# The seven block products of an FFN pair in another order, with the weight sums queued later

## The chip, the cores and the metric

One kernel runs on one core of a Trainium2 chip. The metric is the device time of one execution in microseconds; before the change it is 2068.62 us, the median of three executions (2066.19 to 2069.09). The core has five engines that run side by side, each in its own order: TensorE (PE in the profile, its weight loads PEld), VectorE (DVE), ScalarE (ACT), GpSimd (POOL) and SyncE (SP, whose queue issues most transfers from memory). They wait for each other by semaphores.

## The reference

The kernel computes one inference step of a two-layer network on 128 context tokens and 512 latent tokens with 1024 features. Each layer has a mixer (state space and attention in the first layer, a gated linear recurrence in the second) and then a gated convolutional feed-forward part, the FFN, which the change touches:

```
def conv_ffn(h, w_up, conv_w, conv_b, w_down):
    u = dwconv_centred(h @ w_up, conv_w, conv_b)     # width 3, along the tokens
    val, g = jnp.split(u, 2, axis=-1)
    return (jax.nn.silu(g) * val) @ w_down
...
    xp = xp + gp_f * conv_ffn(modulate(rmsnorm(xp, norm_ffn_g[l]), sp_f, sc_f), *fw)
    xs = xs + gs_f * conv_ffn(modulate(rmsnorm(xs, norm_ffn_g[l]), ss_f, scs_f), *fw)
```

w_up is 1024 x 5632 and w_down 2816 x 1024, all in float32. Modulation vectors (shift, scale, gate) come from a further product with w_mod.

## The kernel before, in words

The 644 token columns (128 of context, a gap of 4, 512 of latents) lie along the free dimension, the features on the partitions. Every product keeps float32 accuracy by splitting each operand into a high part (rounded to fp32r) and a low part (the rest) and adding three matmuls: high by high, high by low, low by high (mm3, L472 to L474). A weight block of 128 output features is loaded as a tile wraw, its high part whi is cast on ACT (L113), its low part wlo is subtracted on POOL in pieces of 256 columns (L118).

The 22 blocks of the value half of w_up and the 22 of the gate half are taken in pairs: pair j is block j of either half. The first two are ordinary products. The other 20 of each FFN are computed by up_pair with seven products of half size in place of eight. The block a is cut into a11 and a12 (its first and last four groups of 128 input features), the block b likewise, and DVE forms sums of them: add_up (L141 to L144) writes s2, s3 and s4 into one tile wsum and s1 over the first half of b. ACT casts the high parts shi of s2, s3, s4, and POOL (for s2) or DVE (for s3 and s4) subtracts the low parts slo. The token side has its own sums T1 to T4 (names t24h, t3h and so on), made once. Then

p1 = a11 B11, p2 = a12 B21, p3 = s4 B22, p4 = a22 T4, p5 = s1 T1, p6 = s2 T2, p7 = s3 T3,

each of them twelve matmuls of 128 x 322, into half of a PSUM tile called wide (128 x 1024; one product lies at column 0, the next at column 512, and then a new tile is taken from three that go round). In the kernel before, the order is p1, p6 | p5, p2 | p7, p4 | p3, where a bar stands between tiles. Copies on ACT (L1602 for p1, L1607 for p5) and additions on DVE (L1604, L1609, L1611, L1614, L1616) and POOL (L1612, L1615) put the seven together into u (value) and g (gate). After that come the convolution (ACT L1551, then two fused operations on DVE at L319 for each of u and g), SiLU (ACT L1567), the product of value and gate (L1562) and its split into hidh and hidl (L509, L513).

The order on PE in each FFN is: two pairs, then six times a down block and three pairs, then the last down block. A down block is eight products of three hidden tiles with w_down, and DVE adds each to the running state X at L319. In the first FFN products for the modulation vectors of the second layer stand between the pieces (M.step).

The program is written out by Python before it runs: the position of each instruction on its engine is the moment at which the Python code emits it. A counter k.clock advances by one with every three matmuls of a half product (tick); after(n, f) emits f when the counter is n further on, and W.ahead(1) emits the next piece of weight work when there are buffers for it. Three wraw, three whi/wlo and four shi/slo buffers go round; wsum is one. pump() asks for the next weight block as soon as the code has given a wraw buffer free. The class Weights holds the lists of pieces for a pair: before, add_up, block a, s2, s3, block b, s4.

Of the kernel before, what the change touches and what calls it, by code (L numbers as in the profile page):

```python
# [44 lines left out]
AHEAD = 3  # L45
N_HID, N_FT = 4, 5
# [37 lines left out]
class Weights:  # L84
# [6 lines left out]
    def __init__(self, nc, pool, items):  # L91
        self.nc, self.pool, self.items = nc, pool, items
        self.loaded = self.freed = self.queued = self.next = 0
        self.raw, self.parts, self.pieces = {}, {}, []
        self.n_raw, self.n_part, self.n_sum = 3, 3, 4
        self.n_w = self.n_s = 0
        self.sums = self.over = None
        self.limit = len(items)

    def pump(self):  # L100
        while self.loaded < min(len(self.items), self.freed + self.n_raw, self.limit):
            ap, kt, w, _ = self.items[self.loaded]
            t = self.pool.tile([128, 8, 128], F32, name="wraw", tag="wraw", bufs=self.n_raw)[:, :kt, :w]
            self.nc.sync.dma_start(t, ap.rearrange("(k p) c -> p k c", p=128))
            self.raw[self.loaded] = t
            self.loaded += 1
# [16 lines left out]
    def block(self, i):  # L123
        raw = self.raw.pop(i)
        if self.items[i][3] == "held":
            hi, lo = (self.over.tile(list(raw.shape), F32R, name=f"{p}{i}") for p in ("hi", "lo"))
            self.nc.scalar.copy(hi, raw)
            for k0 in range(0, raw.shape[1], 2):
                q = slice(k0, min(raw.shape[1], k0 + 2))
                self.nc.gpsimd.tensor_sub(lo[:, q], raw[:, q], hi[:, q].bitcast(F32))  # L130
            self.parts[i] = hi, lo
        else:
            low = self.nc.vector if self.items[i][3] == "vector" else self.nc.gpsimd
            self.parts[i] = self.split(self.pool, raw, "w", self.n_part, low)
        self.freed += 1

    def add_up(self, i):
        a, b = self.raw[i], self.raw[i + 1]
# [11 lines left out]
    def ahead(self, n=100):  # L150
        self.pump()
        for _ in range(n):
            if not self.pieces:
# [4 lines left out]
                if kind == "pair":  # L158
                    if not self.sums or self.loaded < i + 2:
                        return  # L160
                    self.pieces = [(0, lambda: self.add_up(i)), (1, lambda: self.block(i)),
                                   (2, lambda: self.sum_part(i, 0)), (2, lambda: self.sum_part(i, 1)),
                                   (1, lambda: self.block(i + 1)), (2, lambda: self.sum_part(i, 2))]
# [6 lines left out]
            what, f = self.pieces[0]  # L170
            if (what == 1 and self.n_w == self.n_part) or (what == 2 and self.n_s == self.n_sum):
                return
# [6 lines left out]
    def upto(self, i):  # L179

        was = None
        while was != (self.queued, len(self.pieces)) and (self.queued <= i or self.pieces):
            was = self.queued, len(self.pieces)
            self.ahead(1)

    def get(self):
        for _ in range(8):
            if self.next not in self.parts:
                self.ahead(1)
# [4 lines left out]
    def get_pair(self):  # L194
        i = self.next
        while self.queued < i + 2 or (self.queued == i + 2 and self.pieces):
            self.ahead(1)
# [45 lines left out]
def tile_hybrid_step(ctx: ExitStack, tc: tile.TileContext, a, o):  # L243
# [193 lines left out]
    k.bg, k.events, k.clock, k.count = [], [], 0, 0  # L437

# [1060 lines left out]
    def ffn(l, final=None):  # L1499
        with ExitStack() as st:  # L1500
# [78 lines left out]
            def up_pair(j):  # L1579
# [20 lines left out]
                p6 = product(s2, T2, 0, 1)  # L1600
                g, u = tmp(), tmp()
                nc.scalar.copy(g[:, L], p1)  # L1602
                p5 = product(s1, T1)
                nc.vector.tensor_add(u[:, R], p6, g[:, L])  # L1604
                p2 = product(a12, B21, 1)
# [3 lines left out]
                nc.vector.tensor_add(u[:, L], p2, g[:, L])  # L1609
                p4 = product(a22, T4, 1)  # L1610
                nc.vector.tensor_add(g[:, R], p7, u[:, R])  # L1611
                nc.gpsimd.tensor_add(u[:, R], u[:, R], x5)  # L1612
                p3 = product(s4, B22, 0, 1)
                nc.vector.tensor_add(g[:, L], p4, g[:, R])  # L1614
# [369 lines left out]
```

## Time and profile before

| | us |
|---|---|
| median of three executions | 2068.62 |
| the profiled execution | 2074.41 |
| its span, first to last instruction | 2071.4 |
| PE busy | 1885.9 (91%) |
| DVE busy | 1421.0 (69%) |
| POOL busy | 1157.9 (56%) |
| ACT busy | 967.5 (47%) |
| mean granted clock of PE | 0.961 of full speed |

The times in rows are from one execution, the profiled one, counted in microseconds from the start of its span. A row of the timeline gives start, duration, engine, line, operation, output and inputs, and in brackets the idle time of the engine before it and the instruction that ended that idle time. The matmuls of PE overlap one another, so that the distance of two starts, not the duration, is what one costs. Forty pairs run: twenty in the first FFN (about 823 to 1267 us) and twenty in the second (about 1601 to 2019 us).

### The profile page before, as it was taken

Reading aid. Unit: us, or ns where it says so; the run is one execution under the profiler, and the core shown is the slowest. Engines: PE = TensorE matmul, PEld = TensorE weight load, DVE = VectorE, ACT = ScalarE, POOL = GpSimd, SP = SyncE. Lnnn points to the kernel's source line nnn. Section 1 sums busy time; section 2 is a strip of 40 time slices with the busy share of each in tenths; the row PEclk is TensorE's granted clock in tenths of the full one; section 3 lists DMA queues with packets and bytes.
Section 4 is the critical chain, followed back from the end, with each engine's and each line's share of the span. In section 5 each row is a group of like instructions: output and inputs, shape, how many; then the busy total and the mean of one; then the engine's idle time right before and its main releaser. Section 6 shows DMA issues by size and latency. Waiting matters only on the chain. (4 is left out here: it accounts for less than half of the span.)

```text
span 2071.4 us, 33556 instructions
## 1 busy us (share of the span) xinstructions
PE 1885.9 (91%) x12601; PEld 1721.9 (83%) x12601; DVE 1421.0 (69%) x2446; ACT 967.5 (47%) x1679; POOL 1157.9 (56%) x1496
## 2 busy tenths in 40 slices
PE   6878889999999999899999998988789899999997
PEld 4667768888887889788899998977689899999986
DVE  3477764665666347777777776778857777777875
ACT  3454443455545325433434434587726443444445
POOL 3235544333325344566567776468665578776772
PEclk9889999999999999999999999999889899999999
DMA  9554432112113351345543222212121122222221
GB/s 255 179 167 145 143 117 84 49 50 56 39 49 115 100 165 59 97 156 184 154 125 101 85 85 81 59 39 56 41 62 52 46 68 83 85 80 70 62 82 71
DMA packets 255576, 196.58 MB, mean 95 GB/s; under 512 B 13837, under 2 KB 233816, under 8 KB 255288
## 3 DMA queue, kind: packets, MB, share of 16 engines
q1 hardware_dynamic: 249784, 183.94, 29.6%
q0 software_dynamic: 2528, 7.13, 1.5%
q10 hardware_dynamic: 3104, 3.38, 0.5%
q8 instruction: 99, 1.62, 0.3%
q14 instruction: 61, 0.50, 0.1%
HBM read 187.50 MB, written 6.92 MB: 94 GB/s over the span
## 5 line engine op out<-in xcount | busy, mean ns | idle before, releaser
L118 POOL TENSOR_TENSOR wlo<-wraw,whi 128x256 fp32r<-128x256 f32 (+1 forms) x803 | 678.3, 874 | 560.1 <-ACT whi L113 496.3
L472 PE MATMUL wide<-hhi,whi 128*128 128x322 f32 (+4 forms) x1072 | 358.4, 334 | 25.0 <-DVE X L319 16.8
L473 PE MATMUL wide<-hlo,whi 128*128 128x322 f32 (+4 forms) x1072 | 344.2, 321 | 8.2 <-DVE hlo L513 8.0
L474 PE MATMUL wide<-hhi,wlo 128*128 128x322 f32 (+4 forms) x1072 | 341.6, 319 | 3.6 <-POOL wlo L118 3.6
L113 ACT CAST whi<-wraw 128x1024 fp32r<-128x1024 f32 (+1 forms) x259 | 217.2, 840 | 148.4 <-PE wide L474 72.0
L472 PEld LDWEIGHTS wide<-hhi,whi 128*128 128x128 f32 x1072 | 211.2, 197 | 44.1 <-ACT shi L113 16.9
L472 PE MATMUL gh<-hhi,whi 128*128 128x322 f32 (+3 forms) x688 | 232.5, 338 | 8.7 <-ACT zt L1179 8.7
L473 PEld LDWEIGHTS wide<-hlo,whi 128*128 128x128 f32 x1072 | 210.6, 197 | 14.1 <-DVE hlo L513 10.0
L473 PE MATMUL gh<-hlo,whi 128*128 128x322 f32 (+3 forms) x688 | 217.1, 315 | 1.3 <-DVE hlo L513 1.0
L474 PE MATMUL gh<-hhi,wlo 128*128 128x322 f32 (+3 forms) x688 | 216.3, 314 | 0.0
L474 PEld LDWEIGHTS wide<-hhi,wlo 128*128 128x128 f32 x1072 | 211.0, 197 | 4.2 <-POOL wlo L118 4.2
L319 DVE SCALAR_TENSOR_TENSOR ft<-ft,PC 128x643 f32<-128x643 f32 x160 | 167.2, 1066 | 42.7 <-ACT ft L1551 40.8
L472 PE MATMUL wide<-hidh,whi 128*128 128x322 f32 (+2 forms) x600 | 191.3, 319 | 1.1 <-DVE ft L1609 1.1
L473 PE MATMUL wide<-hidl,whi 128*128 128x322 f32 (+2 forms) x600 | 186.9, 311 | 0.8 <-DVE hidl L513 0.8
L474 PE MATMUL wide<-hidh,wlo 128*128 128x322 f32 (+2 forms) x600 | 186.9, 311 | 0.0
L472 PEld LDWEIGHTS gh<-hhi,whi 128*128 128x128 f32 (+1 forms) x688 | 131.8, 192 | 34.1 <-issue 21.2
L319 DVE SCALAR_TENSOR_TENSOR X<-wide,modc,X 128x128 f32<-128x128 f32 (+3 forms) x276 | 128.1, 507 | 30.2 <-PE wide L474 30.2
L1551 ACT ACTIVATE ft<-ft,PC 128x644 f32<-128x644 f32 x80 | 73.9, 926 | 145.6 <-DVE ft L1616 135.5
L473 PEld LDWEIGHTS gh<-hlo,whi 128*128 128x128 f32 (+1 forms) x688 | 131.5, 191 | 2.4 <-DVE hlo L513 1.2
L474 PEld LDWEIGHTS gh<-hhi,wlo 128*128 128x128 f32 (+1 forms) x688 | 131.3, 191 | 0.6
L113 ACT CAST shi<-wsum 128x512 fp32r<-128x512 f32 x120 | 72.8, 617 | 123.0 <-DVE wsum L143 111.4
L472 PEld LDWEIGHTS wide<-hidh,whi 128*128 128x128 f32 x600 | 113.6, 189 | 14.5 <-issue 6.6
(380 smaller groups left out, 4632.1 us busy)
## 6 DMA issues: line engine op xcount, KB each, us to landing
wraw<-in_ffn_w_up_dram SPq DMA_DIRECT2D x88, 512.0 KB
mraw<-in_w_mod_dram SPq DMA_DIRECT2D x80, 512.0 KB
wraw<-in_ssd_attn_w_in_dram SPq DMA_DIRECT2D x42, 512.0 KB
wraw<-in_ffn_w_down_dram SPq DMA_DIRECT2D x96, 192.0 KB
E<-ad SPq DMA_DIRECT2D x16, 640.0 KB
mraw<-in_w_mod_dram SPq DMA_DIRECT2D x32, 256.0 KB
wraw<-in_ssd_attn_w_out_dram SPq DMA_DIRECT2D x16, 512.0 KB
wraw<-in_lru_w_in_dram SPq DMA_DIRECT2D x16, 512.0 KB
```

The costliest lines, as they stand in the source:

```text
L113: self.nc.scalar.copy(hi, src)
L118: low.tensor_sub(lo[:, q], src[:, q], hi[:, q].bitcast(F32))
L319: nc.vector.scalar_tensor_tensor(out, in0, scalar, in1, op0=op0, op1=op1, **kw)
L472: nc.tensor.matmul(ps[:whi.shape[-1], p0:p0 + c1 - c0], whi, xhi[:, c0:c1], start=start, stop=False)
L473: nc.tensor.matmul(ps[:whi.shape[-1], p0:p0 + c1 - c0], whi, xlo[:, c0:c1], start=False, stop=False)
L474: nc.tensor.matmul(ps[:whi.shape[-1], p0:p0 + c1 - c0], wlo, xhi[:, c0:c1], start=False, stop=stop)
L1551: after(at, lambda: nc.scalar.activation(out, u, AF.Identity, scale=par(cw, 2 * NF + t), bias=par(cb, t)))
```

## The change

The seven products are computed in the order p1, p2 | p4, p6 | p5, p7 | p3. The copy of p1 is emitted right after p1, the addition of p2 right after p2, the copy of p5 right after p5, and the addition of p4 before p3. In Weights, the pieces of a pair come as block a, add_up, block b, s2, s3, s4; add_up is emitted at the earliest 12 ticks after the request for block b (LANDING), unless the pair is needed at once; the buffer of block a is given free in add_up.

```
+LANDING = 12
...
             self.raw[self.loaded] = t
+            self.asked[self.loaded] = self.clock()
             self.loaded += 1
...
-    def block(self, i):
-        raw = self.raw.pop(i)
+    def block(self, i, whole=True):
+        raw = self.raw.pop(i) if whole else self.raw[i]
...
+        self.freed += whole
+
+    def add_up(self, i):
+        a, b = self.raw.pop(i), self.raw[i + 1]
         self.freed += 1
-
-    def add_up(self, i):
-        a, b = self.raw[i], self.raw[i + 1]
...
-                    if not self.sums or self.loaded < i + 2:
+                    if not self.sums or self.loaded <= i:
                         return
-                    self.pieces = [(0, lambda: self.add_up(i)), (1, lambda: self.block(i)),
-                                   (2, lambda: self.sum_part(i, 0)), (2, lambda: self.sum_part(i, 1)),
-                                   (1, lambda: self.block(i + 1)), (2, lambda: self.sum_part(i, 2))]
+                    self.pieces = [(1, lambda: self.block(i, False)), (0, lambda: self.add_up(i)),
+                                   (1, lambda: self.block(i + 1)), (2, lambda: self.sum_part(i, 0)),
+                                   (2, lambda: self.sum_part(i, 1)), (2, lambda: self.sum_part(i, 2))]
...
             what, f = self.pieces[0]
+            if what == 0:
+                last = self.queued - 1
+                if self.loaded <= last or (not now and self.clock() < self.asked[last] + LANDING):
+                    return
...
+    W.clock = lambda: k.clock
...
                 p1 = product(a11, B11)
-                p6 = product(s2, T2, 0, 1)
                 g, u = tmp(), tmp()
                 nc.scalar.copy(g[:, L], p1)
-                p5 = product(s1, T1)
+                p2 = product(a12, B21, 1)
+                nc.vector.tensor_add(u[:, L], p2, g[:, L])
+                p4 = product(a22, T4)
+                p6 = product(s2, T2, 0, 1)
                 nc.vector.tensor_add(u[:, R], p6, g[:, L])
-                p2 = product(a12, B21, 1)
+                p5 = product(s1, T1, 1)
                 x5 = pool.tile([128, NT2], F32, name="x5", tag="x5", bufs=1)
                 nc.scalar.copy(x5, p5)
                 p7 = product(s3, T3, 0, 1)
-                nc.vector.tensor_add(u[:, L], p2, g[:, L])
-                p4 = product(a22, T4, 1)
                 nc.vector.tensor_add(g[:, R], p7, u[:, R])
                 nc.gpsimd.tensor_add(u[:, R], u[:, R], x5)
+                nc.vector.tensor_add(g[:, L], p4, g[:, R])
                 p3 = product(s4, B22, 0, 1)
-                nc.vector.tensor_add(g[:, L], p4, g[:, R])
                 nc.gpsimd.tensor_add(g[:, R], g[:, R], x5)
                 nc.vector.tensor_add(u[:, R], u[:, R], p3)
                 nc.gpsimd.memset(g[:, NP:S0], 0.0)
```

The remaining hunks pass now=True where a pair or a block is needed at once. No instruction is added or taken away on any engine; only places change. Line numbers shift by three to nine: after the change the casts are L116, POOL's differences L121, DVE's L123, add_up L145 to L148, the fused operation L327, mm3 L481 to L483, the convolution L1560, the copy of p1 L1610, the addition of p2 L1612, the copy of p5 L1618, the additions of p7, p4 and p3 L1620, L1622 and L1625.

On PE, in the second pair of the last group of three, this is where p1 ends and the next product begins. Before (the names end in numbers of their own; hhi4 is the fifth block of the tokens' high part, and what a row waits for stands in brackets):

```order
L472 MATMUL wide_20096<-hhi3_77,whi_19948 128x322
L473 MATMUL wide_20096<-hlo3_85,whi_19948 128x322
L474 MATMUL wide_20096<-hhi3_77,wlo_19949 128x322
L472 MATMUL wide_20096<-t24h0_15659,shi_19969 128x322
L473 MATMUL wide_20096<-t24l0_15663,shi_19969 128x322
L474 MATMUL wide_20096<-t24h0_15659,slo_19970 128x322 [waits Pool_49]
L472 MATMUL wide_20096<-t24h1_15660,shi_19969 128x322
L473 MATMUL wide_20096<-t24l1_15664,shi_19969 128x322
```

and now:

```order
L481 MATMUL wide_20089<-hhi3_77,whi_19943 128x322
L482 MATMUL wide_20089<-hlo3_85,whi_19943 128x322
L483 MATMUL wide_20089<-hhi3_77,wlo_19944 128x322
L481 MATMUL wide_20089<-hhi4_78,whi_19943 128x322 [waits Activation_49]
L482 MATMUL wide_20089<-hlo4_86,whi_19943 128x322
L483 MATMUL wide_20089<-hhi4_78,wlo_19944 128x322 [waits Pool_49]
L481 MATMUL wide_20089<-hhi5_79,whi_19943 128x322
L482 MATMUL wide_20089<-hlo5_87,whi_19943 128x322
```

Behind p1 stood p6, whose weights are the sums shi; now p2 stands there, in the same tile wide as p1, and its first matmul carries a wait for ACT: the instruction waited for is the copy of p1 (L1610), which reads that tile. The first matmul of p7 has such a wait for the copy of p5 (L1618).

On DVE, in a steady group of the second FFN, the end of a down block, where X takes the products of its fifth, sixth and seventh output block (the eighth comes later). Before:

```order
L319 SCALAR_TENSOR_TENSOR X_73<-wide_17784,modc1_113,X_73 128x128
L319 SCALAR_TENSOR_TENSOR X_73<-wide_17784,modc1_113,X_73 128x512
L141 TENSOR_TENSOR wsum_17812<-wraw_17749,wraw_17782 128x512
L142 TENSOR_TENSOR wraw_17782<-wraw_17782 128x512
L143 TENSOR_TENSOR wsum_17812<-wraw_17782,wraw_17749 128x512
L144 TENSOR_TENSOR wsum_17812<-wraw_17749,wsum_17812 128x512
L319 SCALAR_TENSOR_TENSOR X_73<-wide_17817,modc1_113,X_73 128x128
L319 SCALAR_TENSOR_TENSOR X_73<-wide_17817,modc1_113,X_73 128x512
L120 TENSOR_TENSOR slo_17853<-wsum_17812,shi_17852 128x512
L319 SCALAR_TENSOR_TENSOR X_73<-wide_17856,modc1_113,X_73 128x128
L319 SCALAR_TENSOR_TENSOR X_73<-wide_17856,modc1_113,X_73 128x512
```

and now:

```order
L327 SCALAR_TENSOR_TENSOR X_73<-wide_17784,modc1_113,X_73 128x128
L327 SCALAR_TENSOR_TENSOR X_73<-wide_17784,modc1_113,X_73 128x512
L327 SCALAR_TENSOR_TENSOR X_73<-wide_17812,modc1_113,X_73 128x128
L327 SCALAR_TENSOR_TENSOR X_73<-wide_17812,modc1_113,X_73 128x512
L145 TENSOR_TENSOR wsum_17840<-wraw_17749,wraw_17782 128x512
L146 TENSOR_TENSOR wraw_17782<-wraw_17782 128x512
L147 TENSOR_TENSOR wsum_17840<-wraw_17782,wraw_17749 128x512
L148 TENSOR_TENSOR wsum_17840<-wraw_17749,wsum_17840 128x512
L327 SCALAR_TENSOR_TENSOR X_73<-wide_17847,modc1_113,X_73 128x128
L327 SCALAR_TENSOR_TENSOR X_73<-wide_17847,modc1_113,X_73 128x512
L123 TENSOR_TENSOR slo_17883<-wsum_17840,shi_17882 128x512
L123 TENSOR_TENSOR slo_17887<-wsum_17840,shi_17886 128x512
```

The four operations of add_up for the next pair (tile wsum) have moved behind one more addition to X, that of the sixth block. The first tile wide of the next pair is the one that the sixth block's product lay in, its second the seventh's, its third the eighth's.

On ACT, from the last casts ahead of the first copy of a group of three pairs to the copy of the second pair. Before:

```order
L113 CAST whi<-wraw 128x1024
L113 CAST shi<-wsum 128x512
L1602 COPY ft<-wide 128x322
L113 CAST shi<-wsum 128x512
L1607 COPY x_18665<-wide 128x322
L113 CAST whi<-wraw 128x1024
L113 CAST shi<-wsum 128x512
L113 CAST whi<-wraw 128x1024
L1551 ACTIVATE ft<-ft,PC 128x644
L113 CAST shi<-wsum 128x512
L1551 ACTIVATE ft<-ft,PC 128x644
L1602 COPY ft<-wide 128x322
```

and now:

```order
L116 CAST whi<-wraw 128x1024
L1610 COPY ft<-wide 128x322
L116 CAST whi<-wraw 128x1024
L116 CAST shi<-wsum 128x512 x2
L1618 COPY x_18688<-wide 128x322
L116 CAST shi<-wsum 128x512
L116 CAST whi<-wraw 128x1024
L1560 ACTIVATE ft<-ft,PC 128x644 x2
L1610 COPY ft<-wide 128x322
```

The casts of the pair's second block (whi) and of its sums (shi) stand in another order around the copies. The copy of p1 of the second pair stands behind both convolutions of the first pair, before and now.

## Rows read from the trace of the kernel before

**Rows 1.** The page, busy time, share and instructions of each engine.

```profile
PE 1885.9 (91%) x12601; PEld 1721.9 (83%) x12601; DVE 1421.0 (69%) x2446; ACT 967.5 (47%) x1679; POOL 1157.9 (56%) x1496
```

**Rows 2.** Windows: length, then busy (count) PE, PEld, DVE, ACT, POOL, clock, DMA.

```profile
1791.00:1854.00 63.00, 59.68 (x397) 58.98 (x397) 49.39 (x68) 26.12 (x42) 46.01 (x56) 1.00 0.26 76
...
896.00:967.00 71.00, 68.80 (x498) 61.48 (x499) 54.85 (x90) 27.89 (x44) 46.95 (x59) 1.00 0.52 161
```

**Rows 3.** Waits: engine, line, what was waited for: total us, times, longest.

```profile
ACT ft L1551 <- DVE ft L1616: 135.5, 40, 4.4
...
PE wide L472 <- DVE X L319: 22.6, 16, 2.7
```

**Rows 4.** Timeline of PE, second FFN, a steady group of three pairs.

```profile
1790.99 0.39 PE L472 MATMUL wide<-hhi,whi 128*128 128x322 f32 x1 [2.14 <-DVE X L319]
...
1799.41 0.39 PE L472 MATMUL wide<-t3h,shi 128*128 128x322 f32 x1 [1.05 <-DVE X L319]
...
1804.70 0.30 PE L474 MATMUL wide<-hhi,slo 128*128 128x322 f32 x1
...
1815.82 0.39 PE L472 MATMUL wide<-hhi,shi 128*128 128x322 f32 x1 [0.15 <-DVE ft L1604]
...
1817.52 0.31 PE L474 MATMUL wide<-hhi,slo 128*128 128x322 f32 x1
```

**Rows 5.** Timeline of DVE, the same group.

```profile
1786.41 0.92 DVE L141 TENSOR_TENSOR wsum<-wraw 128x512 f32<-128x512 f32 x1 [3.88 <-DMA wraw<-in_ffn_w_up_dram]
...
1789.85 1.00 DVE L319 SCALAR_TENSOR_TENSOR X<-wide,modc,X 128x128 f32<-128x128 f32 x2
...
1807.91 0.48 DVE L1616 TENSOR_TENSOR ft<-ft,wide 128x322 f32<-128x322 f32 x1
...
1815.20 0.48 DVE L1604 TENSOR_TENSOR ft<-wide,ft 128x322 f32<-128x322 f32 x1
...
1822.12 0.49 DVE L1616 TENSOR_TENSOR ft<-ft,wide 128x322 f32<-128x322 f32 x1 [1.11 <-POOL ft L1612]
```

**Rows 6.** Timeline of PE, first FFN, fourth and sixth group.

```profile
1109.45 0.39 PE L472 MATMUL wide<-t3h,shi 128*128 128x322 f32 x1 [0.55 <-DVE X L319]
...
1227.35 0.61 PE L472 MATMUL wide<-hhi,whi 128*128 128x322 f32 x1 [2.71 <-DVE X L319]
```

**Rows 7.** Timeline of PE and ACT, a copy that waited only for PE.

```profile
1636.59 0.31 PE L474 MATMUL wide<-hhi,wlo 128*128 128x322 f32 x1
...
1636.94 0.43 ACT L1607 COPY x<-wide 128x322 f32<-128x322 f32 x1 [0.39 <-PE wide L474]
```

**Rows 8.** Timeline of ACT, the group of rows 4.

```profile
1790.28 1.04 ACT L113 CAST whi<-wraw 128x1024 fp32r<-128x1024 f32 x1
...
1791.75 1.05 ACT L113 CAST whi<-wraw 128x1024 fp32r<-128x1024 f32 x1
...
1808.43 0.93 ACT L1551 ACTIVATE ft<-ft,PC 128x644 f32<-128x644 f32 x1 [4.14 <-DVE ft L1616]
...
1809.77 0.92 ACT L1551 ACTIVATE ft<-ft,PC 128x644 f32<-128x644 f32 x1
1810.60 0.41 ACT L1602 COPY ft<-wide 128x322 f32<-128x322 f32 x1
```

**Rows 9.** Timeline of PE and DVE, end of the second pair of the second FFN.

```profile
1641.92 0.31 PE L474 MATMUL wide<-hhi,slo 128*128 128x322 f32 x1
...
1642.34 0.49 DVE L1616 TENSOR_TENSOR ft<-ft,wide 128x322 f32<-128x322 f32 x1 [0.83 <-PE wide L474]
```

**Rows 10.** Windows of PE alone: length, busy (matmuls), clock, DMA share, GB/s.

```profile
1728.12:1731.50 3.38, 3.38 (x14) 0.57 0.54 158
1791.00:1794.40 3.40, 3.40 (x23) 1.00 0.54 154
```

**Rows 11.** Timeline of PE and ACT, first pair of the second FFN.

```profile
1607.92 0.64 PE L472 MATMUL wide<-t24h,shi 128*128 128x322 f32 x1 [4.21 <-ACT shi L113]
...
1615.61 0.42 ACT L1602 COPY ft<-wide 128x322 f32<-128x322 f32 x1
```

More of the change, by code (lines that the diff above doesn't have):

```diff
@@ L98, in __init__ @@
         self.limit = len(items)
+        self.clock, self.asked = (lambda: 0), {}
     def pump(self):
@@ L148, in sum_part, with ahead @@
             self.split(self.sums, self.s[:, n], "s", self.n_sum, self.nc.vector if n else self.nc.gpsimd))
-    def ahead(self, n=100):
+    def ahead(self, n=100, now=False):
         self.pump()
@@ L183, in upto @@
             was = self.queued, len(self.pieces)
-            self.ahead(1)
+            self.ahead(1, True)
     def get(self):
@@ L188, in get @@
             if self.next not in self.parts:
-                self.ahead(1)
+                self.ahead(1, True)
         p = self.parts.pop(self.next)
@@ L196, in get_pair @@
         while self.queued < i + 2 or (self.queued == i + 2 and self.pieces):
-            self.ahead(1)
+            self.ahead(1, True)
         return self.get(), self.get(), self.parts.pop((i, "s"))
```

## The prediction

> **What bounds the kernel now.** I read the page's busy times first: PE is busy 91% of the span, every other engine 69% or less [rows 1]. So the end is set by how many matmuls PE issues and by the gaps between them; the change leaves the number as it is. Next the windows: a steady group of the second FFN (a down block and three pairs) takes 63 us, with 397 matmuls and PE busy for 59.68 us; DVE is busy 49.39, POOL 46.01, ACT 26.12 us [rows 2]. One matmul costs 59.68 / 397 = 0.15 us, a product of twelve 1.8 us. So about 3.5 us a group can be won, and no other engine is full; a queue matters only where PE waits for it. Then the waits: PE waited 22.6 us for DVE's additions to X, 16 times [rows 3]. The timeline gives the places. PE stands 2.14 us before the first pair of the group and 1.05 us before its p7, both for X [rows 4]; the addition that ends the first stands behind add_up, which had waited 3.88 us for its block to land [rows 5]. With the slower first matmul each costs 0.15 us more: 2.3 and 1.2. Before p3 of the second pair 0.3 us go [rows 4]. Together 3.8 us a group. Last the ACT queue: its convolutions waited 135.5 us for the last addition of the pair before, 40 times, 4.4 us at most [rows 3]. Nothing on PE waited for that, so far.
>
> **What goes.** The additions of X for the sixth and the eighth block now stand ahead of add_up, and p3's tile waits for the addition of p2, which has four products' time. All three stalls should go: -3.8 us for each of the six groups of the second FFN. In the first FFN the last three groups lost less: 0.55 us at one p7, up to 2.71 us at a start [rows 6]. The third group there lies between; with the slow clock behind the two longer stalls (below) I take 3.2 on the mean. In its first three groups, with modulation products in between, PE is idle 71 - 68.8 = 2.2 us [rows 2], and I count 1.2 of it.
>
> **What comes.** The order shows the point that decides: p1 and p2 share a tile, and so do p5 and p7. The copies of p1 and p5 are now emitted between the two, so the first matmul of p2 waits on a semaphore for ACT's copy, and that of p7 likewise. Before, PE waited only at the borders of tiles, where the reader was a product or two behind. Two new waits a pair, 80 in all.
>
> The least one costs: a copy starts 0.35 us after the last matmul's start and takes 0.43 [rows 7]; PE starts 0.14 us after its releaser ends (1815.20 + 0.48 = 1815.68, against 1815.82) [rows 4, 5]. That is 0.92 us from the last matmul, of which 0.15 would have passed anyway: 0.77 us. For p7, with ACT nearly free, I take 0.8 to 0.85.
>
> For p2 the queue of ACT counts. In the first pair of a group the copy stands behind the casts of the sums and of the next pair's block a. These ended at 1792.80, with one cast of 1.04 us among them [rows 8] that is now done earlier: 1791.8. The copy and the restart add 0.4 and 0.14: 1792.3. PE without its start stall would begin at 1790.99 - 2.3 = 1788.7 and end p1 at 1790.5. Stall 1.8 us, and 0.3 for the low parts of the sums, which POOL now takes up behind block b.
>
> In the second and third pair the copy stands behind both convolutions of the pair before, and these behind its last addition on DVE. From that addition's end to the copy's end it is 1808.39 to 1811.01 here, with a cast of 0.6 between the two convolutions that has moved away [rows 5, 8]; so 0.04 + 0.84 + 0.84 + 0.42 + 0.14 = 2.3 us to PE's restart, less the 1.8 of p1: the stall is the lateness of the last addition plus 0.5. That lateness is 1808.39 - 1804.85 = 3.54 us in the first pair and 1822.61 - 1817.67 = 4.94 in the second [rows 4, 5]; at its least 1642.83 - 1642.07 = 0.76 [rows 9]. It should shrink, since add_up of the next pair but one no longer stands in DVE's queue ahead of it, but POOL's addition still stands behind the two pieces of a sum's low part. For the first pair I take 2.5, in the middle; for the second, with a lighter queue, 1.25. The stalls of p2 are then 3.0 and 1.75.
>
> A group: 1.8 + 0.3 + 0.8 + 3.0 + 0.85 + 1.75 + 0.85 = 9.35 us added. Least: 0.77 + 2 x 1.26 + 3 x 0.77 = 5.6. Most, with the old lateness: 1.8 + 0.3 + 0.8 + 4.0 + 0.85 + 5.4 + 0.85 = 14.0, and 2.3 of the start stall kept.
>
> The transfers: a block is asked for in another place by one piece, on a queue with a share of 0.26 [rows 2]. I count nothing; pairs of 12.5 us cover it, and if a landing is late, it delays add_up and is in the "most".
>
> **The sum.** Second FFN: 6 x (9.35 - 3.8) = 33.3. First FFN, last three groups: 3 x (9.35 - 3.2) = 18.5. First three: the modulation products between pairs ((68.8 - 59.7) / 11 pieces = 0.8 us each [rows 2]) shorten three of the waits by 0.75 each: 3 x (7.1 - 1.2) = 17.7. The two pairs at the start of each FFN: there PE waited 4.21 us for the sums, and the copy of p1 came at 1615.61, behind casts of the tokens [rows 11]. Now the sums are in time, but p2 waits for that copy instead, twelve us after p1's end; what was spread over three stalls is one. I count +1 each, between -4 and +4. Lastly the clock. The same start stall was followed by a granted clock of 0.57 at 1728 (most of that stretch at 1.2 of 2.4 GHz) and of 1.00 at 1791: 14 matmuls in place of 23, or 9 x 0.15 = 1.35 us lost [rows 10]. I counted the slow stretch behind four of the twelve group starts. The 24 new stalls of 1.8 and 3.0 us would by that rate have it eight times, 11 us; half of it would be hidden in the next wait: +6. Sum 33.3 + 18.5 + 17.7 + 2 + 6 = +77.5 us on the profiled execution's 2074.4, or 2151.9; the median of the runs stands 0.28% below that execution, so 2146 us.
>
> **A rule beside it.** The two products of a tile lie at columns 0 and 512 of 1024 float32, that is in different banks. The Trainium skill, "PSUM — Partial Sum Buffer", section "Summary: rules for kernel authors", advises to read PSUM under a running matmul from another bank and to guard by bank. By that rule p2 could run beside the copy, and the change would only take stalls away. The order shows the semaphore all the same: the program guards the tile, not the bank, so I give this little. No row here shows PE writing one half of a tile while ACT reads the other.
>
> **Rivals.** (1) The waits cost nothing, since PE doesn't stop for them, and the stalls go: 6 x 3.8 + 3 x 3.2 + 3 x 1.2 and 4 for each start = 44 us less, 2074.4 - 44 = 2030, as a median 2025. For it: all stalls of rows 4 have their cause moved. Against: the wait stands in the row of p2. Chance 0.06. (2) Only the latencies count, because PE's delay lets the other engines catch up: 6 x (5.6 - 3.8) + 3 x (5.6 - 3.2) + 3 x (4.6 - 1.2) - 8 = +20 (4.6 where modulation products shorten two of the waits to 0.77), so 2089. For it: 49 of 63 us on DVE; against: the order, not the load, makes the lateness. Chance 0.16. (3) Every new stall of p2 in the groups, 36, lowers the clock: 36 x 1.35 - 6 = 43 more, 2189. For it: 0.57 after 2.2 us of idling. Against: 1.00 after as much [rows 10]. Chance 0.11, with what else is late. (4) Gain and loss cancel, the latencies as in (2) and the starts of the two FFNs giving back 14 each instead of 4: 2069, chance 0.03. The forecast has 0.64. The side changes where the new waits cost less than 3.8 us a group, that is where p2's stalls are under half a microsecond each; the latency alone is 0.77.
>
> Range: from rival 2 to nearly rival 3, 2087 to 2190; the bounds of the sum (12.5 us a group) would reach 2215, which I leave out with rival 1. A difference under 0.2% can't be told from none in these runs. Faster by more: 0.07; within: 0.03; slower by more: 0.90.
>
> **What would show it.** Right: in the waits PE waits for ACT's copies L1610 and L1618, eighty times, 70 to 130 us in all; the idle time for X falls under 6 us; the first pair of a group starts without a gap; p2 of the second pair waits 2 to 4 us, its convolutions on ACT ending just ahead. Wrong: p2 starts 0.15 us after p1, or the waits for copies are all under 0.9 us (rival 2), or the granted clock falls in most groups (rival 3).

## The result and the profile after

The changed kernel takes 2137.81 us, the median of four runs (2135.14 to 2140.04), against 2067.46 us for the kernel before on the same chips: the ratio is 1.0327, with a 95% interval of 1.0310 to 1.0345. It is slower by 70 us; 2146 us was forecast.

The page's first part, after:

```profile
PE 1898.7 (89%) x12601; PEld 1722.2 (81%) x12601; DVE 1440.1 (67%) x2446; ACT 973.6 (46%) x1679; POOL 1168.1 (55%) x1496
```

The counts are those of [rows 1]; the span is 2138.1 us in place of 2071.4, and PE is busy 13 us longer; the rest of the 67 us is waiting. The waits of PE and of the convolutions, after (total us, times, longest):

```profile
ACT ft L1560 <- DVE ft L1625: 101.6, 40, 4.5
PE wide L481 <- ACT ft L1610: 73.8, 40, 14.1
PE wide L481 <- ACT x L1618: 27.8, 40, 1.5
```

PE waits forty times for the copy of p1 and forty times for the copy of p5, 101.6 us in all, which the kernel before did not do once. The wait for additions to X at L319, 22.6 us in [rows 3], is gone from the FFN. A steady group of the second FFN answers to the first of [rows 2] and to [rows 4]. Its window first (length, busy and count of PE, PEld, DVE, ACT, POOL, then clock, DMA share, GB/s):

```profile
1838.00:1906.00 68.00, 61.68 (x395) 60.09 (x394) 50.38 (x67) 26.53 (x41) 46.42 (x56) 0.97 0.24 70
```

Then PE's timeline there (start, length, instruction, in brackets the idle time before it and what ended it): the group's first matmul and every one of the three pairs that had waited 0.5 us or more:

```profile
1837.81 0.31 PE L481 MATMUL wide<-hhi,whi 128*128 128x322 f32 x1
...
1840.27 0.42 PE L481 MATMUL wide<-hhi,whi 128*128 128x322 f32 x1 [0.52 <-ACT ft L1610]
1848.47 0.41 PE L481 MATMUL wide<-t3h,shi 128*128 128x322 f32 x1 [0.81 <-ACT x L1618]
1856.44 0.41 PE L481 MATMUL wide<-hhi,whi 128*128 128x322 f32 x1 [2.34 <-ACT ft L1610]
1865.85 0.42 PE L481 MATMUL wide<-t3h,shi 128*128 128x322 f32 x1 [0.52 <-ACT x L1618]
1873.11 0.42 PE L481 MATMUL wide<-hhi,whi 128*128 128x322 f32 x1 [1.62 <-ACT ft L1610]
1880.99 0.41 PE L481 MATMUL wide<-t3h,shi 128*128 128x322 f32 x1 [0.52 <-ACT x L1618]
```

The first row is the first matmul of the group: it has no idle time, where 2.14 us stood in [rows 4]. The six others are p2 and p7 of the first, second and third pair. From the first matmul of one group to that of the next, five groups take 340.9 us after and 314.1 before, 5.4 us more each. ACT's queue at the second pair answers to [rows 8]:

```profile
1838.27 1.05 ACT L116 CAST whi<-wraw 128x1024 fp32r<-128x1024 f32 x1
1839.79 0.43 ACT L1610 COPY ft<-wide 128x322 f32<-128x322 f32 x1 [0.47 <-PE wide L483]
...
1854.33 1.74 ACT L1560 ACTIVATE ft<-ft,PC 128x644 f32<-128x644 f32 x2 [2.30 <-DVE ft L1625]
1855.98 0.40 ACT L1610 COPY ft<-wide 128x322 f32<-128x322 f32 x1
```

In the first pair the copy waits for PE alone (0.47 us idle), the casts are done in time. In the second it comes behind both convolutions, and these behind the last addition of the first pair, DVE's L1625, which ends at 1854.30:

```profile
1833.59 0.68 DVE L145 TENSOR_TENSOR wsum<-wraw 128x512 f32<-128x512 f32 x1
...
1853.81 0.49 DVE L1625 TENSOR_TENSOR ft<-ft,wide 128x322 f32<-128x322 f32 x1 [1.35 <-POOL ft L1621]
```

The pair ends at 1852.14, so this is 2.2 us late (2.5 was taken; 3.54 before). add_up for the first pair starts at 1833.59 and waits for no transfer, which [rows 5] had at 3.88 us. The first pair of either FFN waits once, for the copy that stands behind the casts of the tokens:

```profile
841.44 0.63 PE L481 MATMUL wide<-hhi,whi 128*128 128x322 f32 x1 [11.35 <-ACT ft L1610]
...
1652.06 0.64 PE L481 MATMUL wide<-hhi,whi 128*128 128x322 f32 x1 [14.14 <-ACT ft L1610]
```

### The profile page after: what moved, and what is told of

The parts are those of the page before. It is cut to its first block, busy times and chain, and to the rows that moved or that the text cites. A ratio compares the mean times of both kernels' runs of the same rounds, so it can differ in the third digit from the quotient of the medians.

```text
span 2138.1 us, 33465 instructions
## 1 busy us (share of the span) xinstructions
PE 1898.7 (89%) x12601; PEld 1722.2 (81%) x12601; DVE 1440.1 (67%) x2446; ACT 973.6 (46%) x1679; POOL 1168.1 (55%) x1496
## 3 DMA queue, kind: packets, MB, share of 16 engines
q8 instruction: 99, 1.62, 0.3%
## 5 line engine op out<-in xcount | busy, mean ns | idle before, releaser
L121 POOL TENSOR_TENSOR wlo<-wraw,whi 128x256 fp32r<-128x256 f32 (+1 forms) x803 | 699.6, 899 | 631.8 <-ACT whi L116 598.5
L481 PE MATMUL wide<-hhi,whi 128*128 128x322 f32 (+4 forms) x1072 | 361.3, 337 | 81.4 <-ACT ft L1610 73.8
L116 ACT CAST whi<-wraw 128x1024 fp32r<-128x1024 f32 (+1 forms) x259 | 217.5, 841 | 307.0 <-PE wide L482 124.7
L483 PE MATMUL wide<-hhi,wlo 128*128 128x322 f32 (+4 forms) x1072 | 342.1, 319 | 3.7 <-POOL wlo L121 3.7
L481 PEld LDWEIGHTS wide<-hhi,whi 128*128 128x128 f32 x1072 | 210.3, 196 | 108.7 <-ACT ft L1610 84.3
L481 PE MATMUL gh<-hhi,whi 128*128 128x322 f32 (+3 forms) x688 | 233.5, 339 | 8.8 <-ACT zt L1188 8.7
L483 PE MATMUL gh<-hhi,wlo 128*128 128x322 f32 (+3 forms) x688 | 217.3, 316 | 0.0
L483 PEld LDWEIGHTS wide<-hhi,wlo 128*128 128x128 f32 x1072 | 210.9, 197 | 4.2 <-POOL wlo L121 4.1
L481 PE MATMUL wide<-hidh,whi 128*128 128x322 f32 (+2 forms) x600 | 190.7, 318 | 0.0
L327 DVE SCALAR_TENSOR_TENSOR ft<-ft,PC 128x643 f32<-128x643 f32 x160 | 165.8, 1057 | 31.7 <-ACT ft L1560 30.3
L483 PE MATMUL wide<-hidh,wlo 128*128 128x322 f32 (+2 forms) x600 | 186.5, 311 | 0.0
L327 DVE SCALAR_TENSOR_TENSOR X<-wide,modc,X 128x128 f32<-128x128 f32 (+3 forms) x276 | 129.7, 510 | 54.7 <-PE wide L483 54.7
L481 PEld LDWEIGHTS gh<-hhi,whi 128*128 128x128 f32 (+1 forms) x688 | 132.2, 192 | 34.7 <-issue 21.2
L483 PEld LDWEIGHTS gh<-hhi,wlo 128*128 128x128 f32 (+1 forms) x688 | 131.6, 191 | 1.0
L481 PEld LDWEIGHTS wide<-hidh,whi 128*128 128x128 f32 x600 | 113.0, 188 | 13.2 <-issue 9.5
L1294 DVE TENSOR_REDUCE mx<-wide 128x1 f32<-128x768 f32 (+1 forms) x80 | 62.2, 819 | 81.4 <-PE wide L1290 80.7
L1560 ACT ACTIVATE ft<-ft,PC 128x644 f32<-128x644 f32 x80 | 69.9, 918 | 101.6 <-DVE ft L1625 101.6
```

The costliest lines, as they stand in the source:

```text
L116: self.nc.scalar.copy(hi, src)
L121: low.tensor_sub(lo[:, q], src[:, q], hi[:, q].bitcast(F32))
L327: nc.vector.scalar_tensor_tensor(out, in0, scalar, in1, op0=op0, op1=op1, **kw)
L481: nc.tensor.matmul(ps[:whi.shape[-1], p0:p0 + c1 - c0], whi, xhi[:, c0:c1], start=start, stop=False)
L483: nc.tensor.matmul(ps[:whi.shape[-1], p0:p0 + c1 - c0], wlo, xhi[:, c0:c1], start=False, stop=stop)
L1294: nc.vector.reduce_max(mx[:, c:c + 1], s[c][:, :w], axis=AX, negate=True)
```

## The experiments

What stood to be tested: are the waits for the copies the loss, or do they stand in front of another one? Lines shift from kernel to kernel; the text says which operation a line is. "New Weights" means the changed class (block a, add_up after 12 ticks, block b, s2, s3, s4), "new order" the new order of products.

**The copies later, one alone of the two parts, and the convolution later.** Four kernels, timed against 2070.35 us of the kernel before.

```
e1_late (on the changed kernel)
                 p1 = product(a11, B11)
-                nc.scalar.copy(g[:, L], p1)
                 p2 = product(a12, B21, 1)
+                nc.scalar.copy(g[:, L], p1)
...
-                nc.scalar.copy(x5, p5)
                 p7 = product(s3, T3, 0, 1)
+                nc.scalar.copy(x5, p5)
```

> The changed kernel with the copy of p1 emitted after p2 and the copy of p5 after p7; nothing else differs from it. Theory (the two new waits of PE for these copies are the loss, and the rest of the change is a gain): the 101.6 us that PE idled for L1610 and L1618 go, with 0.15 us for each restart and the slow clock behind the longer of them, and only part of the two long waits at the start of each FFN comes back as waits for sums: 2137.8 becomes about 2030 (2015 to 2045), below the kernel before. Rival (the order of the products, or the sums that are queued later, costs the time, and the wait for the copies only stands in front of another wait): it stays above 2100.

Measured 2110.11 us, 1.0192 (1.0173 to 1.0212). Faster than the changed kernel by 28 us, far from 2030. The waits for copies are gone, and two others have come, for the additions of p7 (L1620 here) and p2 (L1612):

```profile
PE wide L481 <- DVE ft L1620: 46.2, 12, 4.2
PE wide L481 <- DVE ft L1612: 23.7, 12, 6.0
```

```profile
1837.73 0.41 PE L481 MATMUL wide<-hhi,shi 128*128 128x322 f32 x1 [1.43 <-DVE ft L1612]
1843.92 0.64 PE L481 MATMUL wide<-hhi,whi 128*128 128x322 f32 x1 [4.16 <-DVE ft L1620]
```

The first is p3 of the second pair, the second the first matmul of the third pair. So my expectation fell, and the time is the rival's (above 2100): most of the copies' waits stood in front of waits for DVE.

```
e2_weights: the kernel before with the new Weights; up_pair as before
e3_products: the kernel before with the new order, copies and additions of up_pair; Weights as before
```

> The kernel before with the change to the class Weights alone (add_up 12 ticks behind the request, block b split ahead of the sums); the products and copies in the old order. Theory: no wait for copies; the start stall for X goes (2.3 us a group), but p6 is still the second product, and its sum's low part now stands behind block b on POOL, about 4 us, so that p6 waits 2 to 4 us: between 2060 and 2090, 2075 as the middle. Rival (queueing the sums later is itself the loss of the changed kernel): above 2110.

> The kernel before with the new order of products, copies and additions alone; Weights as before. Theory: the waits for the copies are there in full, 80 of them, and the start stall of 2.3 us a group stays: 2137.8 + 10 to 20, about 2150 (2135 to 2170). Rival (the order of products is harmless, the late sums cost the time): 2060 to 2080.

e2_weights measured 2116.30 us, 1.0216 (1.0193 to 1.0239), outside the range of the theory (2060 to 2090) and in that of the rival (above 2110). The wait is all the same the one that the theory named, only larger: PE waits for the low part of s2, which POOL makes behind block b.

```profile
PE wide L483 <- POOL slo L121: 54.5, 26, 3.8
```

e3_products measured 2199.20 us, 1.0618 (1.0587 to 1.0650), 129 us above the kernel before, where 80 had been expected; the rival's 2060 to 2080 is farther off still. The waits for the copies of p1 (L1601) and p5 (L1609) are all there:

```profile
PE wide L472 <- ACT ft L1601: 98.7, 40, 14.0
PE wide L472 <- ACT x L1609: 20.8, 40, 0.5
```

Each part alone is slower, and together they lose less (70 us) than the products alone (129): the new Weights give back 59 us under the new order.

```
e4_conv (on the changed kernel)
-FFN = (4, 3, 4, 3, 4, 4)
+FFN = (4, 3, 4, 3, 4, 5)
```

> The changed kernel with the convolution of the gate half emitted one tick later (k.pace[5] 5 in place of 4), so that the copy of p1 of the next pair stands behind one convolution on ACT, not two. Theory (the wait of p2 in the second and third pair is the last addition's lateness plus ACT's queue): 0.84 us less at each of the 24 such waits, and less of the slow clock: 2137.8 - 20 = 2118 (2108 to 2128). Rival (only the latency of a copy counts, or p2 waits for something else): 2138, no change.

Measured 2146.13 us, 1.0364 (1.0346 to 1.0383): 8 us slower, not 20 faster. The local claim holds: p2 of the second pair waits 1.52 us in place of 2.34, the 0.82 of one convolution. But p7 of that pair now waits 2.97 us where it waited 0.52, since the copy of p5 stands behind the SiLU, and this behind the convolution that was put off:

```profile
1856.40 0.41 PE L481 MATMUL wide<-hhi,whi 128*128 128x322 f32 x1 [1.52 <-ACT ft L1610]
1866.77 0.41 PE L481 MATMUL wide<-t3h,shi 128*128 128x322 f32 x1 [2.97 <-ACT x L1618]
```

```profile
1865.14 0.74 ACT L1576 ACTIVATE ft<-ft 128x644 f32<-128x644 f32 x1 [5.19 <-DVE ft L327]
...
1866.30 0.42 ACT L1618 COPY x<-wide 128x322 f32<-128x322 f32 x1
```

**What the waits for copies cost by themselves.** Timed against 2071.63 us, with two more that follow e1_late and e2_weights.

```
e7_late_oldw: e3_products with both copies late, as in e1_late
e8_early: the kernel before, its own order, with (the two copies' old lines go)
                 p1 = product(a11, B11)
+                nc.scalar.copy(g[:, L], p1)
                 p6 = product(s2, T2, 0, 1)
...
                 p5 = product(s1, T1)
+                nc.scalar.copy(x5, p5)
                 p2 = product(a12, B21, 1)
```

> The kernel before (Weights as before) with the new order of products, and the copies emitted late, that of p1 after p2 and that of p5 after p7: e3_products without its waits for copies. There PE idled 119.5 us for copies. Theory 1 (those waits are time lost in full): 2199 - 119 - 12 for the restarts = about 2065 (2050 to 2085). Theory 2, after e1_late (they stand in front of DVE's queue, in which the additions of a pair come behind the sums of the next; half or more comes back as waits for L1612 and L1620): 2120 to 2160.

> The kernel before, old order of products, old Weights; only the copy of p1 is emitted ahead of p6 and the copy of p5 ahead of p2, so that PE waits for both in the middle of a tile. Theory (those two waits by themselves cost what e3_products lost): 0.7 us at least for each of 80, and about 3 at the first of the second and third pair, 8.7 a group less the 1.5 of stalls that they hide: 2070 + 85 = 2155 (2120 to 2215), with 80 waits of PE for ACT in its list. Rival (the new order of products is what costs, not the place of the copies): 2065 to 2085.

e8_early measured 2192.56 us, 1.0591 (1.0571 to 1.0612), 121 us slower with nothing moved but the two copies (and the allocation of x5), and inside the range of the theory:

```profile
PE wide L472 <- ACT ft L1601: 95.0, 40, 14.0
PE wide L472 <- ACT x L1605: 32.9, 40, 2.6
```

e7_late_oldw measured 2090.00 us, 1.0085 (1.0055 to 1.0115), between the two theories and nearer to the first: without these waits e3_products loses 109 us less (the two were timed on different chips, their ratios are 1.0618 and 1.0085). Of what is left of the new order's loss, 18 us, the largest wait stands where it stood in e1_late, at the addition of p7 (L1611 here):

```profile
PE wide L472 <- DVE ft L1611: 25.8, 14, 2.3
```

The order of the program fits this, though no run changed it alone. A pair takes four tiles of three, and the next pair's first product gets the tile whose last reader was emitted first. In the old order that is the tile of p2, the fourth product; in the new order it is that of p7, the sixth, so that DVE has 1.8 us in place of 5.4 until PE wants it.

```
e9_s2_first (on e2_weights)
                     self.pieces = [(1, lambda: self.block(i, False)), (0, lambda: self.add_up(i)),
-                                   (1, lambda: self.block(i + 1)), (2, lambda: self.sum_part(i, 0)),
-                                   (2, lambda: self.sum_part(i, 1)), (2, lambda: self.sum_part(i, 2))]
+                                   (2, lambda: self.sum_part(i, 0)), (2, lambda: self.sum_part(i, 1)),
+                                   (1, lambda: self.block(i + 1)), (2, lambda: self.sum_part(i, 2))]
e10_late_s2 (on e1_late): the order a, add_up, s2, block b, s3, s4
```

> The kernel e2_weights (old products, add_up 12 ticks behind the request) with the pieces in the order block a, add_up, s2, s3, block b, s4: the sums' parts stand ahead of block b again. Theory (the loss of e2_weights is p6 waiting for the low part of s2, which POOL makes behind block b; 54.5 us, 26 times): 2116 - 54 = 2062, with the start stall for X gone (2045 to 2070). Rival (the delay of the sums by 12 ticks is itself the loss): above 2095.

> The kernel e1_late with the pieces in the order block a, add_up, s2, block b, s3, s4: the low part of s2 stands ahead of block b on POOL. In e1_late the next pair's add_up waited 1.8 us on DVE for that part (there is one wsum), and the addition of p2 (L1612), for which p3 waits, stands behind it. Theory: the 1.45 us before p3 go and part of the 4.15 us for L1620 too, 2 us a group: 2110 - 25 = 2085 (2070 to 2100). Rival (L1612 and L1620 are late for the length of DVE's queue alone): 2105 to 2115.

e9_s2_first measured 2079.09 us, 1.0037 (1.0016 to 1.0057): 37 of the 46 us of e2_weights are gone with the order of s2 and block b, and the expected 2062 is missed, because a wait for the addition of p6 (L1613) has come, behind the third pair's add_up and three operations of the convolution:

```profile
1803.08 0.81 DVE L145 TENSOR_TENSOR wsum<-wraw 128x512 f32<-128x512 f32 x1
...
1807.24 3.95 DVE L327 SCALAR_TENSOR_TENSOR ft<-ft,PC 128x643 f32<-128x643 f32 x3
...
1812.52 0.48 DVE L1613 TENSOR_TENSOR ft<-wide,ft 128x322 f32<-128x322 f32 x1
```

```profile
1813.14 0.61 PE L481 MATMUL wide<-hhi,shi 128*128 128x322 f32 x1 [3.14 <-DVE ft L1613]
```

e10_late_s2 measured 2112.71 us, 1.0207 (1.0178 to 1.0236), the rival's figure. The wait for L1612 fell from 23.7 to 9.0 us, as the theory had it; the wait for L1620 stayed, and a new one for block b on POOL took the rest:

```profile
PE wide L481 <- DVE ft L1620: 47.0, 13, 4.1
PE wide L483 <- POOL wlo L121: 19.6, 11, 4.5
PE wide L481 <- DVE ft L1612: 9.0, 11, 3.7
```

**add_up held back until an addition of the pair is emitted.** Timed against 2069.25 us.

```
e11_hold (on e9_s2_first)
-                if self.loaded <= last or (not now and self.clock() < self.asked[last] + LANDING):
+                if self.loaded <= last or (not now and (self.hold or self.clock() < self.asked[last] + LANDING)):
...
+                W.hold = True
                 p1 = product(a11, B11)
...
                 p5 = product(s1, T1)
                 nc.vector.tensor_add(u[:, R], p6, g[:, L])
+                W.hold = False
e12_hold2: the same, with that addition and W.hold = False ahead of p5
```

> The kernel e9_s2_first, in which PE's one large wait in a group is 3.1 us before p3 of the second pair, for the addition of p6 (L1613 there): on DVE it stands behind the add_up of the third pair. Here add_up of the next pair is held back until that addition is emitted. Theory (the order of DVE's queue is the loss, not its load): the wait goes, with its restart and the slow clock behind it, 4 us in each of 12 groups, some of it coming back as waits for the sums, which are later: 2079 - 48 + 14 = 2045 (2030 to 2060), below the kernel before. Rival (DVE has more work than a pair lasts, so that the wait comes back at the next border of a tile): 2065 to 2085.

> As e11_hold, with the addition of p6 emitted right behind the copy of p1, one product earlier, so that add_up of the next pair and its sums come one product earlier too. Theory as for e11_hold, with about 1 us less waiting for sums in each group: 2035 (2022 to 2055). Rival: 2065 to 2085.

e11_hold measured 2055.71 us, 0.9932 (0.9917 to 0.9947): the fastest kernel of the study, 14 us below the kernel before, in the range that was given. A group takes 62.1 us, the clock stays at 1.00, and the longest wait left in it is 1.2 us for the addition of p2 (L1620 here):

```profile
PE wide L481 <- DVE ft L1620: 12.1, 11, 1.4
```

e12_hold2, one product earlier, measured 2077.08 us, 1.0033 (1.0015 to 1.0050), the rival's figure. PE waits again for the addition of p2, for which the next pair's first product needs the tile:

```profile
PE wide L481 <- DVE ft L1620: 38.4, 12, 4.4
```

add_up stands ahead of that addition in both kernels. In e12_hold2 the low part of a sum (L123) stands ahead of it too, and waits 1.70 us for its cast; in e11_hold that part comes behind the addition.

```profile
1820.16 0.69 DVE L123 TENSOR_TENSOR slo<-wsum,shi 128x512 fp32r<-128x512 f32 x1 [1.70 <-ACT shi L116]
...
1821.51 0.49 DVE L1620 TENSOR_TENSOR ft<-wide,ft 128x322 f32<-128x322 f32 x1
```

```profile
1822.15 0.39 PE L481 MATMUL wide<-hhi,whi 128*128 128x322 f32 x1 [3.98 <-DVE ft L1620]
```

So in the old order one product's difference in the place of add_up is worth 21 us, by what comes to stand ahead of the additions in DVE's queue. The same hold under the new order, with late copies and with the changed kernel's early ones, timed against 2071.03 us:

```
e13_late_hold (on e1_late), e14_after_hold (on the changed kernel): W.hold = True ahead of p1,
                 nc.vector.tensor_add(u[:, L], p2, g[:, L])
+                W.hold = False
```

> The kernel e1_late (new order of products, copies emitted late) with add_up of the next pair held back until the addition of p2 is emitted. In e1_late PE waited 69.9 us for the additions of p2 and p7, which stand on DVE behind that add_up (four operations, 4.2 us). Theory (what took the place of the copies' waits is the place of add_up in DVE's queue): the 1.45 us before p3 go, and some 1.5 of the 4.1 before the third pair, with the slow clock behind it: 2110 - 12 x 3.5 = 2070 (2055 to 2090). Rival (it is the amount of DVE's work in a pair, whatever its order): 2095 to 2112.

> The changed kernel, early copies and all, with the same hold on add_up. Theory: the waits for the copies depend on ACT's queue and the convolutions, not on add_up, and stay, about 100 us: 2138 becomes 2130 (2118 to 2140), and e14 less e13 is what the copies' waits cost where nothing else stands behind them, about 60 us. Rival (the copies' waits matter no more than the 28 us between the changed kernel and e1_late): e14 less e13 is 30 us or less.

e13_late_hold measured 2103.95 us, 1.0160 (1.0143 to 1.0177), in the rival's range. The wait for p2's addition is gone, and it has gone over to the addition of p7 (L1622 here), 5.5 us in a group:

```profile
PE wide L481 <- DVE ft L1622: 64.1, 14, 5.7
```

Between the last additions of the first and of the second pair DVE is busy for 14.8 us of 16.6 there (window of DVE alone: length, busy and count, clock, DMA share, GB/s), whereas PE needs 12.5 us for a pair:

```profile
1823.40:1840.00 16.60, 14.83 (x18) 0.83 0.08 25
```

That amount alone does not decide. In e11_hold, in the old order, DVE is busy 13.59 of 16.80 us between the same two additions, and PE loses only the 1.2 us:

```profile
1787.80:1804.60 16.80, 13.59 (x19) 1.00 0.14 42
```

e14_after_hold measured 2135.92 us, 1.0314 (1.0299 to 1.0330), the changed kernel's time, with 97.6 us of waiting for copies. e14 less e13 is 32 us, where about 60 was expected and 30 or less by the rival; the changed kernel less e1_late is 28. Under the new Weights and the new order that is all that comes back when the copies are emitted late, for waits for DVE's additions take the place of the waits for copies.

## Why the prediction was right, point by point

*The direction and the mechanism* were right: the first matmul of p2 and of p7 waits for ACT's copy in all forty pairs, 101.6 us (70 to 130 were named), and the start stall is gone. e8_early shows the mechanism alone, in the old order. The number is nearer than its parts: the new stalls were sized too long and the starts of the two FFNs too short, and the two partly cancel, which is luck. And the waits that the sum adds up are not what their removal gives back (see the rivals below).

*The sum.* +77.5 us was forecast for the profiled execution, +65.6 came (+66.7 from first to last instruction). The span is taken apart by the first matmul of each stretch on PE. The groups of the second FFN gave +31.5 (33.3 and a part of the 6 for the clock), those of the first +32.0 (its first three 15.7 against 17.7, its last three 16.3 against 18.5). The two starts gave +3.9 and +3.2 (1 each); the stretches before the first FFN, between the two and behind the last pair, which were not counted, gave -1.4, -0.1 and -2.5.

*What goes.* The waits for X went in all six groups. The 3.8 us were read from one group, though: in two of the six (those that start at 1728.12 and 1853.92) no stall stood before p7, and the slow clock behind the start stall in its place. The reason given, that X's additions would stand ahead of add_up, is what the timeline shows, with one more that I had not counted: add_up no longer waits for its transfer.

*What comes.* The six stalls of the group above are 6.33 us of idling and six restarts of 0.15, 7.2 us, where 9.35 were forecast. *p2 of the first pair* was sized at 1.8 us and 0.3 more, and cost 0.67 (0.52 idle and the restart): since add_up starts 4.2 us ahead of the group, the casts are through when the copy's turn comes. This is the term that was off most, 1.4 us in nearly every group. *p2 of the second pair*: 3.0 forecast, 2.34 idle and 2.5 with the restart; *of the third*: 1.75 forecast, 1.62 idle and 1.77 with the restart; *p7*: 0.8 to 0.85 forecast, 0.67 mostly. The least cost was sized at 0.77 and came out at 0.67 because PE starts 0.05 us after the copy's end (1839.79 + 0.43 = 1840.22, against 1840.27), where 0.14 had been read from one addition. The rule "lateness of the last addition plus 0.5" gave 2.66 for a lateness of 2.16.

*The clock.* Forecast: eight slow stretches for 24 stalls, 6 us net. It came behind p2 of the second pair in all six groups of the second FFN, and once in the first FFN, behind p2 of a third pair after 1.89 us of idling (last row): seven slow stretches in place of the four behind starts before.

```profile
1856.44:1859.84 3.40, 3.40 (x14) 0.58 0.00 0
1206.68:1210.08 3.40, 3.40 (x23) 1.00 0.00 0
1153.45:1156.85 3.40, 3.40 (x14) 0.56 0.19 58
```

The second of these rows is p2 of the second pair in the first FFN, after 2.33 us of idling: there it stayed at full speed. At 1.35 us each, three more slow stretches are about 4 us, near the 6 forecast.

*The rule beside it.* The copy and p2 did not run side by side, as the order had shown. That they could on this chip no run here tested: the kernels that do without the wait emit the copy later, and it then waits for p2.

*Rivals.* Rival 2 (latency alone) was right for p2 of the first pair and mostly for p7, and wrong for the rest. Rival 3 (the clock) held behind seven of the 36 stalls of p2 in the groups; its sign, a slow clock in most groups, was met by count (7 of 12), but not its 43 us. Rival 4 did not come. Rival 1 gave 2025 us for a change whose waits cost nothing, and rested on a step that the sum uses too: that the stalls removed are won in full. There the prediction had a hole that its own number didn't show. With the waits taken away the time is 2110 us (e1_late) or 2104 (e13_late_hold), about 80 us above that figure: the new order itself needs p7's addition before the next pair may start, and that addition comes late on DVE (5.5 us of PE's waiting in a group of e13_late_hold). What I had read as "49 of 63 us on DVE", room enough, says nothing of when an addition's turn comes. Emitting the copies early costs 121 us in the old order, 109 in the new with the old Weights, and 28 to 32 in the changed kernel, though PE's list shows 98 to 128 us of them each time.

What stays open: why the new Weights give the new order 59 us back (e3_products to the changed kernel). From the first pair to the last down block of both FFNs, e3_products takes 1003.6 us with PE busy 868.7, the changed kernel 945.1 with 841.2. So 31 us of it are idle time, 18 of them in the waits for copies, and 27 are busy time, at a granted clock of 0.96 and 0.93 against 0.98 and 0.96 in the two FFNs. No run changed only the place of the sums. A fourth tile in the rotation, which would give p7's addition time, was not tried, so that this reason for the late start of the next pair is argued, not shown alone.

## What to carry to other kernels

When a line is moved in a program that is ordered as it is written, ask of each reader moved who writes its tile next: a read emitted between two writers of one tile becomes a wait of the second, whatever part of the tile it reads. A wait in the list is worth what stands behind it: 100 us of waiting for copies gave 28 when taken away, since the next engine in line was as late; where it was not, waits of the same kind cost 121. And an engine's busy share does not tell whether it is in time. Between the last additions of two pairs DVE was busy 89% in e13_late_hold, where PE waited 5.5 us for it, and 81% in e11_hold, where PE waited 1.2: look at what stands ahead of the one operation that is waited for, and at how soon its tile is wanted.

## What the runs showed of the hardware that was not expected

Almost the same idle time of PE, 2.33 and 2.34 us at p2 of a second pair, was followed by a granted clock of 1.00 in the first FFN and of 0.58 in the second; after 0.5 us (1840.27) it stayed at 1.00 in the second too (window of the changed kernel, all engines):

```profile
1840.27:1843.67 3.40, 3.40 (x23) 3.40 (x24) 1.59 (x4) 0.00 (x0) 3.40 (x5) 1.00 0.39 116
```

The length of the idle time alone does not decide it in these runs. On DVE the additions of 512 columns for the sums took 0.69 us where POOL stood still and 1.1 where it worked beside them, so that in this pair add_up, held back, was also a third shorter. In e13_late_hold POOL was idle for 3.68 us until 1831.80:

```profile
1829.84 0.69 DVE L146 TENSOR_TENSOR wraw<-wraw 128x512 f32<-128x512 f32 x1
...
1831.80 4.01 POOL L121 TENSOR_TENSOR wlo<-wraw,whi 128x256 fp32r<-128x256 f32 x4 [3.68 <-issue]
```

In e1_late it worked from 1829.44 on:

```profile
1829.44 9.71 POOL L121 TENSOR_TENSOR wlo<-wraw,whi 128x256 fp32r<-128x256 f32 x8
...
1830.03 1.12 DVE L146 TENSOR_TENSOR wraw<-wraw 128x512 f32<-128x512 f32 x1
```
